# A mixture-of-experts stage on one core: rows for experts 4 to 31 fetched from DRAM through a slot table, in place of one-hot matmuls

## The chip, the cores and the metric

The kernel runs on one core of one Trainium2 chip. The metric is device time in microseconds (us) of one execution, lower is better; the time before is the median of three runs. A profile shows one further execution, with its own time.

## The reference, cut to what matters

Two blocks follow each other on 512 tokens of width 1024. The change touches only the end of the second block, the mixture of 32 experts. With `x` the residual stream and `h = rms_norm(x, norm_ffn)`:

```python
g_idx = argmax(softmax(h @ w_router_group))          # one of 4 groups
top_logit, top_idx = top_k(h @ w_router_expert[g_idx], 2)   # 2 of its 8 experts
gate = softmax(top_logit) * p_group[g_idx]
for each chosen expert e of a token:
    hid = silu(h @ w1[e]) * (h @ w3[e])              # 1024 -> 512
    y += gate * (hid @ w2[e])                        # 512 -> 1024
x = x + y
```

So 512 x 2 = 1024 token-expert pairs fall on 32 experts: 32 on average.

## The kernel before, in words

All matmuls run on float32 data that is split in two parts: a high part (`wh`, a cast on ACT, `piece_hi`) and a low part (`wl`, the difference, on DVE, `piece_lo`). An expert's weights come from DRAM as six 1 MB transfers, issued by SP, into a ring of buffers (`raw`, `pre`, `X`). Each transfer holds two *pieces*; an expert has 12 pieces (four each of w1, w3, w2), and the list `pieces` sets the order. For each piece the loop at the end of `build` runs PE's matmuls, with ACT and DVE splitting up to four pieces ahead; one w1 piece of each expert from expert 1 on is used unsplit (`whole`). Each expert has 64 slots (`CAP`) for its tokens. Its input `xg` holds 64 columns of high parts and 64 of low parts.

PE, DVE, ACT and POOL keep the order in which the code is written here (`manual_schedule`). Hooks (`after(i, d, f)`) put an expert's later steps behind a given piece: `s_copy1/3` and `s_add1/3` gather the two column halves, `s_hidden` makes the hidden layer, and `s_combine` (`combine`, L1509) multiplies by the gate into the tile `xs0`, of which there is one, and adds the 64 rows to the output by an indirect transfer on POOL's queue (L1517). Empty slots go to 64 spare rows behind the output.

**Gather.** For four experts at a time, `Gather` makes one-hot matrices on DVE (`start`, L1128), multiplies the token rows `hm` by them on PE (`sums`, `psc<-OH,X`), copies the result into `xg` on ACT and DVE (`step`, L1321 and L1323) and gets gates and row numbers by further small matmuls (`finish`). Group 0 is gathered in the router; the groups 1 to 7 while the last expert of the group ahead runs.

**Router.** For each of four token tiles m, between the matmuls of the last projection (`co`): `r_add`, `r_norm`, `r_rstd`, `r_scale`, `r_high`, `r_low` make the normalised rows and their two parts; `r_transpose`, `r_logits`, `r_choice` (some 12 small DVE operations), `r_place`, `r_place2` and `one_hot` find each token's experts and slots. POOL takes the low parts of the six first pieces and of two tiles.

```python
if e % NE == 3 and n != "w2" and e < 31:
    after(i, 0, lambda e=e: grp[e // NE + 1].step())
```

A loop at the end serves experts with more than 64 tokens; in the profiled execution PE has no instruction behind the last expert's.

## Time and profile before

| | |
|---|---|
| median of 3 runs | 1729.56 us (1728.92 to 1729.67) |
| the profiled execution's own time | 1727.33 us |
| its span, first to last instruction | 1725.4 us |
| PE, DVE, ACT, POOL busy | 95%, 75%, 51%, 10% of the span |
| mean granted TensorE clock | 0.987 |
| DRAM traffic | 336 MB, 308.69 MB of it on SP's queue |

Busy shares are means over stages. Up to about 1140 us the first block, attention and router run; from there to the end the experts do. A matmul's end is modelled and overlaps the next one's start. Times are us from the span's start unless marked ns.

### The profile page before, as it was taken

What the parts mean: (1) busy time and instruction counts of PE and PEld (TensorE: products, weight loads), DVE (VectorE), ACT (ScalarE), POOL (GpSimd) and SP (SyncE); (2) the same over time, 40 slices, a digit from 0 to 9 for tenths busy, and PEclk for the clock granted to TensorE, in tenths of its full rate; (3) what the DMA queues carried; (4) which work ended last, traced back from release to release, by engine and by line L of the source; (5) the groups of instructions that cost most, each with busy time, mean ns of one, the idle gap of its engine ahead of it and who ended that gap; (6) DMA issues with size and microseconds to landing.
All of it is one profiled execution on the core that took longest, in us unless ns stands there. A gap on an engine that the chain in (4) does not pass through costs nothing. (4 is left out here: it accounts for less than half of the span.)

```text
span 1725.4 us, 21422 instructions
## 1 busy us (share of the span) xinstructions
PE 1646.7 (95%) x8035; PEld 1325.1 (77%) x8035; DVE 1297.0 (75%) x1938; ACT 882.2 (51%) x1381; POOL 166.0 (10%) x146
## 2 busy tenths in 40 slices
PE   8999999999999999998999999889999999999995
PEld 6788888888888888887787877677676776777763
DVE  5969996489994465456656554579999999999995
ACT  6533232322223235343554432457878878778784
POOL 1100100000000000003101100320101101011011
PEclk9999999999999999998999999989999999999998
DMA  9932232223222362332212312429999999999994
GB/s 352 317 102 97 80 110 80 98 88 99 100 86 78 119 218 98 122 134 97 74 50 105 116 49 98 171 98 332 364 349 405 350 391 365 348 406 346 389 366 148
DMA packets 97801, 336.24 MB, mean 195 GB/s; under 512 B 6560, under 2 KB 24224, under 8 KB 73376
## 3 DMA queue, kind: packets, MB, share of 16 engines
q1 hardware_dynamic: 89952, 308.69, 47.2%
q0 software_dynamic: 6880, 23.96, 5.3%
q10 hardware_dynamic: 864, 2.21, 0.3%
q8 instruction: 64, 1.05, 0.2%
q14 instruction: 41, 0.34, 0.1%
HBM read 319.89 MB, written 14.94 MB: 194 GB/s over the span
## 5 line engine op out<-in xcount | busy, mean ns | idle before, releaser
L149 ACT CAST wh<-raw 128x1024 fp32r<-128x1024 f32 x174 | 182.0, 1051 | 386.0 <-PE ps L141 340.6
L150 DVE TENSOR_TENSOR wl<-raw,wh 128x1024 fp32r<-128x1024 f32 x174 | 212.4, 1224 | 170.0 <-ACT wh L149 169.1
L141 PE MATMUL pmm<-wh,X 128*128 128x512 f32 (+1 forms) x576 | 188.3, 398 | 2.3 <-ACT jk L784 1.8
L141 PE MATMUL ps<-hH,wl 128*128 128x512 f32 x448 | 175.2, 392 | 0.0
L141 PE MATMUL ps<-hL,wh 128*128 128x512 f32 x448 | 174.6, 390 | 0.5 <-DVE hL L150 0.5
L141 PE MATMUL ps<-hH,wh 128*128 128x512 f32 x448 | 174.5, 389 | 0.0
L487 DVE SCALAR_TENSOR_TENSOR cvo<-apad,cw,cvo 128x512 f32<-128x512 f32 x240 | 170.6, 757 | 0.9
L1257 DVE TENSOR_TENSOR wl<-raw,wh 128x1024 fp32r<-128x1024 f32 x137 | 163.4, 1222 | 3.0 <-ACT wh L1254 2.3
L141 PE MATMUL pmm<-wl,xr 128*128 128x512 f32 x322 | 138.4, 430 | 14.6 <-DVE wl L1257 14.6
L1254 ACT CAST wh<-raw 128x1024 fp32r<-128x1024 f32 x139 | 142.4, 1052 | 0.0
L1257 DVE TENSOR_TENSOR wl<-pre,wh 128x1024 fp32r<-128x1024 f32 x109 | 127.4, 1221 | 5.1 <-ACT wh L1254 5.1
L141 PE MATMUL pmm<-wh,xr 128*128 128x512 f32 x322 | 127.1, 395 | 0.0
L141 PEld LDWEIGHTS pmm<-wh,X 128*128 128x128 f32 x576 | 108.8, 195 | 22.6 <-ACT jk L784 2.0
L141 PE MATMUL ps<-wl,hH 128*128 128x512 f32 x320 | 124.5, 390 | 0.0
L141 PE MATMUL ps<-wh,hH 128*128 128x512 f32 x320 | 124.5, 389 | 0.0
L141 PE MATMUL ps<-wh,hL 128*128 128x512 f32 x320 | 124.5, 390 | 0.0
L141 PE MATMUL pmm<-wl,X 128*128 128x512 f32 (+1 forms) x288 | 114.3, 397 | 0.0
L1517 POOL DMA_INDIRECT out_dram<-xs,ii x31 | 64.2, 2070 | 505.7 <-DVE xs L1516 505.7
L1254 ACT CAST wh<-pre 128x1024 fp32r<-128x1024 f32 x113 | 112.0, 1055 | 0.0
L141 PEld LDWEIGHTS ps<-hL,wh 128*128 128x128 f32 x448 | 84.1, 188 | 18.4 <-DVE hL L150 0.9
L141 PEld LDWEIGHTS ps<-hH,wh 128*128 128x128 f32 x448 | 84.1, 188 | 17.5
L141 PEld LDWEIGHTS ps<-hH,wl 128*128 128x128 f32 x448 | 84.0, 188 | 17.5 <-issue 0.2
(426 smaller groups left out, 3431.2 us busy)
## 6 DMA issues: line engine op xcount, KB each, us to landing
raw<-in_w_dram SPq DMA_DIRECT2D x93, 1024.0 KB, 8.3
pre<-in_w_dram SPq DMA_DIRECT2D x62, 1024.0 KB, 7.7
raw<-in_w_in_dram SPq DMA_DIRECT2D x43, 1024.0 KB, 5.0
X<-in_w_dram SPq DMA_DIRECT2D x31, 1024.0 KB, 7.6
adar<-in_w_ada_dram SPq DMA_DIRECT2D x16, 512.0 KB, 8.5
raw<-in_w_in_dram SPq DMA_DIRECT2D x16, 512.0 KB, 4.5
raw<-in_w_ret_out_dram SPq DMA_DIRECT2D x8, 1024.0 KB, 4.9
raw<-in_w_out_dram SPq DMA_DIRECT2D x8, 1024.0 KB, 5.2
```

The lines of the kernel that those rows point to most:

```text
L141: PE.matmul(o, l, r, start=start, stop=stop)
L149: A.copy(hi, src)
L150: E.tensor_sub(lo, src, hi.bitcast(F32))
L487: V.scalar_tensor_tensor(st["o"], ap[:, j:j + T], cw[:, k, j:j + 1], st["o"], op0=OP.mult, op1=OP.add)
L1254: A.copy(split_of[i][0], raw_of[i])
L1257: E.tensor_sub(split_of[i][1], raw_of[i], split_of[i][0].bitcast(F32))
L1517: G.indirect_dma_start(out=out, out_offset=bass.IndirectOffsetOnAxis(ap=idx[:, :1], axis=0), in_=y[:64, :], in_offset=None, bounds_check=T ...
```

## The change

- The normalised rows (`r_scale` now on ACT with a strided read, `r_gain` on DVE) are also stored to DRAM (`xscr`); their order by feature is set once, so `r_high` and `r_low` read and write without strides.
- The router's lines stand in another order, and POOL no longer takes low parts: DVE does. Pieces 2 and 3 are used unsplit.
- `places` computes for each token and choice its slot, `table` writes row number and gate into the DRAM table `slots` by eight indirect transfers of 128 entries of 8 bytes, and reads the table back into `tb`.
- For experts 4 to 31, `fetch` gets the rows by an indirect transfer (POOL's queue, two experts ahead, two buffers), `turn` transposes them on PE, `parts` splits them on ACT and DVE. Groups 1 to 7 of the one-hot gather are gone.
- The scatters and fetches leave out slots that hold no token. Three buffers that held `hm` join the ring of weight buffers (nine in place of six).

Cut to what matters:

```diff
@@ -236,6 +238,8 @@
     sinT = hp.tile([128, T], F32, name="sinT")
     kscr = dp.tile([128, 2048], F32, name="kscr")
     vscr = dp.tile([128, 2048], F32, name="vscr")
+    xscr = dp.tile([T, D], F32, name="xscr")
+    slots = dp.tile([CAP * 32, 2], F32, name="slots")
...
@@ -1114,10 +1118,15 @@
-    g_ffn = gain(I["norm_ffn_2"].unsqueeze(0))
+    g_ffn = gain(I["gffn"])
     zero = alt("xs")
     V.memset(zero[:64], 0.0)
     G.dma_start(out[T:T + 64, :], zero[:64])
+
+    none = zero[:, 512:512 + CAP * 32 // 64].rearrange("p (s v) -> p s v", v=2)
+    V.memset(none, 0.0)
+    V.memset(none[:, :, 0].bitcast(I32), 1 << 20)
+    G.dma_start(slots.rearrange("(p s) v -> p s v", p=128), none)
     rt = [{} for m in range(NT)]
     rb = []
     NE = 4
@@ -1153,24 +1162,27 @@
         rt[m]["rs"] = sp.tile([128, 1], F32, name="rs1")
         rstd(rt[m]["rs"], rt[m]["ss"], D, 1e-6)
-    def r_scale(m, E=V):
-        rs = rt[m]["rs"]
-        E.scalar_tensor_tensor(rt[m]["xs"], xr[m], rs, g_ffn, op0=OP.mult, op1=OP.mult)
-
-
-    def natural(ap):
-        return ap.rearrange("t (c p k) -> t c p k", c=2, k=4)
     def by_feature(ap):
-        return ap.rearrange("t (c k p) -> t c p k", c=2, k=4)
+        return ap.rearrange("t (c p k) -> t c k p", c=2, k=4)
+
+    def tiles(ap):
+        return ap.rearrange("t (c k p) -> t c k p", c=2, k=4)
+
+    def r_scale(m):
+        A.activation(tiles(rt[m]["xs"]), by_feature(xr[m]), AF.Copy, scale=rt[m]["rs"])
+
+    def r_gain(m):
+        V.tensor_mul(rt[m]["xs"], rt[m]["xs"], g_ffn)
+        nc.scalar.dma_start(xscr[m * 128:m * 128 + 128, :], rt[m]["xs"])
     def r_high(m):
         h = xslot([128, 2, D])
-        A.copy(by_feature(h[:, 0]), natural(rt[m]["xs"]))
+        A.copy(h[:, 0], rt[m]["xs"])
         hm.append(h)
-    def r_low(m, E=V):
-        E.tensor_sub(by_feature(hm[m][:, 1]), natural(rt[m]["xs"]), by_feature(hm[m][:, 0].bitcast(F32)))
+    def r_low(m):
+        V.tensor_sub(hm[m][:, 1], rt[m]["xs"], hm[m][:, 0].bitcast(F32))
     def r_logits(m):
         b = rb[0][:, m * 40:m * 40 + 40]
@@ -1362,87 +1374,85 @@
     rb.append(ppv())
     cb = [pmm(), pmm(), pmm()]
+
+    for i in range(2):
+        piece_hi(i)
+        piece_lo(i, V)
     co(0, cb[0], 0)
     co(0, cb[0], 1)
     r_add(0, cb[0])
     r_norm(0)
     r_rstd(0)
-    piece_hi(0)
-    piece_lo(0, G)
+    co(1, cb[1], 0)
+    co(1, cb[1], 1)
     r_scale(0)
+    r_gain(0)
+    r_add(1, cb[1])
+    r_norm(1)
+    r_rstd(1)
+    r_transpose(0)
+    co(2, cb[2], 0)
     r_high(0)
     r_low(0)
-    co(1, cb[1], 0)
-    co(1, cb[1], 1)
-    r_add(1, cb[1])
-    r_transpose(0)
-    r_norm(1)
-    r_rstd(1)
+    r_logits(0)
     r_scale(1)
-    r_high(1)
-    piece_hi(1)
-    r_low(1)
-    piece_lo(1, G)
-    co(2, cb[2], 0)
+    r_choice(0)
...
+    r_gain(2)
+    r_rstd(3)
+    r_high(2)
+    r_scale(3)
+    g0 = group(0, OH0)
+    for n in ("pg", "pa"):
+        g0.begin(len(g0.begun), pget(n))
     r_choice(2)
-    r_scale(3)
-    piece_hi(4)
-    piece_lo(4, G)
-    r_high(3)
-    r_low(3, G)
-    piece_hi(5)
-    piece_lo(5, G)
     r_logits(3)
-    g0 = group(0, OH0)
-    g0.begin(0, pget("pg"))
+    for n in ("pg", "pa", "py", "py"):
+        g0.begin(len(g0.begun), pget(n))
     r_place(2)
     r_place2(2)
     one_hot(OH0, 2, pm1[:, 2, :NE])
-    for n in ("pg", "py", "py", "pa", "pa"):
-        g0.begin(len(g0.begun), pget(n))
+    r_low(2)
+    for k in range(6):
+        g0.more(g0.begun[k], k, 0, NT - 2)
     r_choice(3)
-    for k in range(2):
-        for l in range(2):
-            g0.more(g0.begun[k], k, l, NT - 2)
+    for k in range(6):
+        g0.more(g0.begun[k], k, 1, NT - 2)
+    r_gain(3)
+    r_high(3)
     r_place(3)
-    for k in range(2, 6):
-        for l in range(2):
-            g0.more(g0.begun[k], k, l, NT - 2)
     r_place2(3)
     one_hot(OH0, 3, pm1[:, 3, :NE])
+    r_low(3)
+    piece_hi(4)
+    piece_lo(4, V)
+    piece_hi(5)
+    piece_lo(5, V)
     p6.close()
     ex = mt_("ex", NT, 4)
     ge = mt_("ge", NT)
@@ -1461,10 +1471,39 @@
+    tb = mt_("tb", 32, 2)
+    dat = mt_("dat", NT, 2, 2)
+    pqv = mt_("pqv", NT, 2)
+    pen = mt_("pen", NT, 2)
+    pi = mt_("pi", NT, 2, dtype=I32)
+
+    def places():
+
+        w32 = late_[:, 384:].rearrange("p (m e) -> p m e", m=NT)
+        V.tensor_sub(el, Mb, o2)
+        for c, o in enumerate((el, o2)):
+            V.tensor_mul(w32, o, pm1)
+            V.tensor_reduce(pqv[:, :, c], w32, AX.X, OP.add)
+        V.tensor_scalar(pen, pqv, float(CAP), float(1 << 20), OP.is_gt, OP.mult)
+        V.tensor_scalar(pqv, pqv, 32.0, -32.0, OP.mult, OP.add)
+        V.tensor_add(pqv, pqv, gi[:, :, :2])
+        V.tensor_add(pqv, pqv, pen)
+        V.tensor_copy(pi, pqv)
+
+    def table():
+        for c, o in enumerate((gs, ge)):
+            V.tensor_copy(dat[:, :, c, 0].bitcast(I32), meta[:, :, 0])
+            V.tensor_copy(dat[:, :, c, 1], o)
+        for m in range(NT):
+            for c in range(2):
+                G.indirect_dma_start(out=slots, out_offset=bass.IndirectOffsetOnAxis(ap=pi[:, m, c:c + 1], axis=0),
+                                     in_=dat[:, m, c, :], in_offset=None, bounds_check=CAP * 32 - 1, oob_is_err=False)
+        for l in range(2):
+            G.dma_start(tb[l * 64:l * 64 + 64], slots.rearrange("(s e) v -> s e v", e=32))
     def up(b, x, k0, w):
@@ -1482,7 +1521,8 @@
     def whole(i):
-        return pieces[i][0] == "w1" and pieces[i][2] == 2 and pieces[i][1] > 0
+        n, e, c = pieces[i]
+        return n == "w1" and (c == 2 or e == 0 and c == 3)
     def down(yb, hd, f, w):
@@ -1515,7 +1555,7 @@
             A.activation(y[:64, c], yb[q][:64], AF.Copy, scale=gate[:64])
             V.scalar_tensor_tensor(y[:64, c], yb[q][64:], gate[64:], y[:64, c], op0=OP.mult, op1=OP.add)
         G.indirect_dma_start(out=out, out_offset=bass.IndirectOffsetOnAxis(ap=idx[:, :1], axis=0),
-                             in_=y[:64, :], in_offset=None, bounds_check=T + 63, oob_is_err=True,
+                             in_=y[:64, :], in_offset=None, bounds_check=T - 1, oob_is_err=False,
                              compute_op=OP.add)
     p6 = ExitStack()
@@ -1523,7 +1563,6 @@
     for n in ("q0", "q1"):
         raws.add((pre2, n, RAW, F32))
     raws.add((lp, "X0", RAW, F32))
-    grp = {0: g0}
     g0.step(4)
     st = [{} for e in range(32)]
     late = {}
@@ -1537,13 +1576,12 @@
             if raws.i == 10 and len(raws.slots) == 8:
                 p6.close()
                 raws.slots, raws.i = [raws.slots[j] for j in (2, 3, 4, 7, 0, 1)], 0
+                raws.slots = [((lp, f"X{j}", RAW, F32),) for j in (1, 2, 3)] + raws.slots
                 xp2 = p6.enter_context(pool("xg2", side="right"))
                 k = wsp.i % len(wsp.slots)
                 wsp.slots, wsp.i = wsp.slots[k:] + wsp.slots[:k], 0
                 wsp_add((xp2, "wh7"), (xp2, "wl7"))
                 wsp.slots = wsp.slots[-1:] + wsp.slots[:-1]
-                xgs.add((xp2, "xg4", [128, KT, 128], F32R))
-                xgs.i = 4
             piece_load(i)
         if not whole(i):
             piece_hi(i)
@@ -1567,9 +1605,38 @@
         st[e]["hd"] = hidden(st[e]["b"])
     def s_combine(e):
-        g = grp[e // NE]
         y = xgs.next().rearrange("p k t -> p (k t)").bitcast(F32) if e == 31 else None
-        combine(st[e]["y"], g.mg[:, e % NE:e % NE + 1], g.ii[:, e % NE:e % NE + 1], y)
+        if e < NE:
+            gate, ids = g0.mg[:, e:e + 1], g0.ii[:, e:e + 1]
+        else:
+            gate, ids = tb[:, e, 1:2], tb[:64, e, 0:1].bitcast(I32)
+        combine(st[e]["y"], gate, ids, y)
+
+    def fetch(o, ids):
+
+        G.indirect_dma_start(out=o, out_offset=None, in_=xscr, in_offset=bass.IndirectOffsetOnAxis(ap=ids, axis=0),
+                             bounds_check=T - 1, oob_is_err=False)
+
+    def turn(x):
+
+        b = pget("pg")
+        for k in range(KT):
+            transpose(b[:, k * 64:k * 64 + 64], x[:, k * 128:k * 128 + 128])
+        return b.rearrange("p (k s) -> p k s", k=KT)
+
+    def parts(b, xg):
+        A.copy(xg[:, :, :64], b)
+        V.tensor_sub(xg[:, :, 64:], b, xg[:, :, :64].bitcast(F32))
+
+    def s_fetch(e):
+        fetch(rows[:64, e % 2], tb[:64, e, 0:1].bitcast(I32))
+
+    def s_turn(e):
+        st[e]["xb"] = turn(rows[:64, e % 2])
+
+    def s_parts(e):
+        st[e]["xg"] = xgs.next()
+        parts(st[e]["xb"], st[e]["xg"])
@@ -1598,22 +1665,29 @@
         while done < len(pieces) and done < i + look:
             prepare(done)
             done += 1
-        g = grp[e // NE]
+        g = g0
         s_ = st[e]
+        if e < NE:
+            s_["xg"] = g.xg[e]
         if i in (1, 2):
             g.step(2)
         if i == 3:
+            places()
             gates()
+        if i == 4:
+            rows = lp.tile([128, 2, D], F32, name="X4")
+            G.memset(rows[:64], 0.0)
+            table()
         if i == 11:
             g.finish()
         if n != "w2":
             if c == 0:
                 s_[n] = pget("pa")
             if whole(i):
-                up_whole(s_[n], g.xg[e % NE], 2 * c, raw_of[i])
+                up_whole(s_[n], s_["xg"], 2 * c, raw_of[i])
             else:
-                up(s_[n], g.xg[e % NE], 2 * c, split_of.pop(i))
+                up(s_[n], s_["xg"], 2 * c, split_of.pop(i))
         else:
             if c == 0:
                 s_["y"] = [pget("pg" if e == 31 else "py") for _ in range(2)]
@@ -1634,13 +1708,12 @@
             after(i, 1, blocks)
             after(i, 5, blocks_before)
-        if e % NE == 2 and n == "w3" and c == 3 and e < 28:
-            grp[e // NE + 1] = group(e // NE + 1)
-            after(i, 1, grp[e // NE + 1].start)
-        if e % NE == 3 and n != "w2" and e < 31:
-            after(i, 0, lambda e=e: grp[e // NE + 1].step())
-            if n == "w3" and c == 3:
-                after(i, 1, grp[e // NE + 1].finish)
+        if n == "w1" and e < 32:
+            if c == 1 and NE <= e + 1 < 32:
+                after(i, 0, lambda e=e: s_turn(e + 1))
+                after(i, 1, lambda e=e: s_parts(e + 1))
+            if c == 3 and NE <= e + 2 < 32:
+                after(i, 0, lambda e=e: s_fetch(e + 2))
         for f in late.pop(i, ()):
             f()
     p8.close()
@@ -1679,8 +1752,9 @@
         ev = nc.sync.value_load(curi[0:1, 0:1], min_val=0, max_val=31)
         ga = Gather(pl, mt2, 2, 1, xgs.next)
         ga.start()
-        ga.step(8)
         ga.finish()
+        fetch(rows[:64, 0], ga.ii[:, 0:1])
+        parts(turn(rows[:64, 0]), ga.xg[0])
         w1, w3, w2 = (I[n][bass.ds(ev, 1)].rearrange("o k n -> (o k) n") for n in ("w1_2", "w3_2", "w2_2"))
         aS = lp.tile([128, 2, 512], F32, name="gain0")
         b = pget("ph")
```

Three places of the order that the code sets.

DVE, at the step from one expert to the next, in the last expert of a group, before (`xs` is the combined output, `xr` the next group's input, the others weight parts):

```order
L1503 TENSOR_TENSOR hs<-hs,ppv 128x256
L150 TENSOR_TENSOR hd<-hs,hd 128x4x64
L1516 SCALAR_TENSOR_TENSOR xs_9740<-ptr,mg,xs_9740 64x512 x2
L1321 CAST xr_9699<-psc 128x128
L1321 CAST xr_9700<-psc 128x128
L1257 TENSOR_TENSOR gain_9764<-raw_9761,xs_9763 128x1024
L1321 CAST xr_9699<-psc 128x128
L1321 CAST xr_9700<-psc 128x128
```

and the same place now, in any expert (`L1629` is `parts`):

```order
L1543 TENSOR_TENSOR hs<-hs,ppv 128x256
L152 TENSOR_TENSOR hd<-hs,hd 128x4x64
L1556 SCALAR_TENSOR_TENSOR xs_9261<-ptr,mg,xs_9261 64x512 x2
L1269 TENSOR_TENSOR wl_9272<-raw_9269,wh_9271 128x1024
L1269 TENSOR_TENSOR wl_9289<-raw_9269,wh_9288 128x1024
L1629 TENSOR_TENSOR xr_9294<-psc,xr_9294 128x8x64
```

One 512-column subtraction in every expert stands in place of sixteen 128-column casts and four one-hot operations in every fourth.

POOL, in the router, before (`wl` are the first pieces' low parts, `X` the tiles' low parts, `rs` the small power for the norm):

```order
L1257 TENSOR_TENSOR wl_8315<-pre_8213,wh_8314 128x1024
L225 TENSOR_TENSOR rs_8381<-rs_8381,mhalf 128x1
L1173 TENSOR_TENSOR X_8385<-xs_8378,X_8385 128x2x128x4
L1257 TENSOR_TENSOR wl_8435<-pre_8215,wh_8434 128x1024
L225 TENSOR_TENSOR rs_8460<-rs_8460,mhalf 128x1
L1257 TENSOR_TENSOR wl_8439<-pre_8215,wh_8438 128x1024
```

POOL has only the `rs` rows there now. Behind them, from piece 4 on, stands the table, with the semaphores that each waits for (DMASW are those of POOL's transfers, each number used in turn):

```order
L1680 MEMSET X_8726 64x2048 [waits DVE_49,PE_49]
L1503 DMA slots<-dat,pi 2048x2 [waits DMASW5_49,DVE_49]
L1503 DMA slots<-dat,pi 2048x2 [waits DMASW6_49,DVE_49]
L1503 DMA slots<-dat,pi 2048x2 [waits DMASW7_49]
L1503 DMA slots<-dat,pi 2048x2 [waits DMASW1_49,DMASW0_49]
...
L1503 DMA slots<-dat,pi 2048x2 [waits DMASW4_49]
L1506 DMA tb<-slots 64x64 [waits DMAHW5_49,DMASW5_49]
L1506 DMA tb<-slots 64x64
L1557 DMA out_dram<-xs_8975,ii 576x1024 [waits DMAHW4_49,DMAHW7_49,DMAHW2_49,DVE_49]
L1617 DMA X_8726<-xscr,tb 64x1024 [waits DMAHW4_49,DMAHW3_49,DMAHW5_49,DMASW6_49,Pool_49]
```

Each write to `slots` waits for the one before it to land, the reading back for the last of them; expert 0's scatter and expert 4's fetch come behind on the same queue.

## Rows read from the trace of the kernel before

**Rows 1.** Windows, the router's end: busy us by engine, clock, DMA share, GB/s.

```profile
core 0: us, PE busy (x) PEld busy (x) DVE busy (x) ACT busy (x) POOL busy (x), PEclk, DMA share, GB/s
1100.00:1150.00 50.00, 36.67 (x203) 33.22 (x203) 36.51 (x92) 21.12 (x36) 19.50 (x9) 0.80 0.37 147
```

**Rows 2.** Windows: four experts (10 to 13) singly, then experts 2 to 30.

```profile
1359.00:1374.70 15.70, 15.45 (x69) 11.07 (x67) 14.98 (x16) 13.36 (x18) 2.26 (x1) 1.00 0.95 354
...
1374.70:1390.30 15.60, 14.52 (x65) 10.60 (x64) 14.89 (x15) 13.26 (x18) 2.26 (x1) 1.00 1.02 396
...
1390.30:1407.30 17.00, 15.95 (x78) 11.84 (x76) 16.28 (x19) 13.32 (x19) 2.25 (x1) 1.00 1.01 410
...
1407.30:1429.80 22.50, 22.15 (x146) 18.67 (x146) 19.66 (x38) 16.63 (x33) 1.40 (x1) 1.00 0.90 337
...
1217.68:1706.62 488.94, 466.43 (x2368) 354.60 (x2366) 454.68 (x577) 392.33 (x572) 58.10 (x29) 1.00 0.95 366
```

**Rows 3.** Waits, 1288 to 1712 us, SP's queue: total us, times, longest.

```profile
SPq L1248 <- DVE wl L1257: 157.9, 72, 4.3
```

**Rows 4.** Timeline of DVE, 1363 to 1374 us: start, us, what, idle before.

```profile
1363.53 4.62 DVE L1257 TENSOR_TENSOR wl<-pre,wh 128x1024 fp32r<-128x1024 f32 x4
...
1368.07 1.22 DVE L1257 TENSOR_TENSOR wl<-raw,wh 128x1024 fp32r<-128x1024 f32 x1
...
1373.07 1.54 DVE L1516 SCALAR_TENSOR_TENSOR xs<-ptr,mg,xs 64x512 f32<-64x512 f32 x2 [0.16 <-ACT xs L1515]
```

**Rows 5.** Groups by form, 1288 to 1712 us, five gathers: busy, mean ns.

```profile
L141 PE MATMUL psc<-OH,X 128*128 128x256 f32 x320 | 47.5, 287 | 1.8 <-ACT xr L1323 1.4 <-ACT xg L1323 0.3
...
L1321 DVE CAST xr<-psc 128x128 fp32r<-128x128 f32 x64 | 16.2, 285 | 2.7 <-ACT xr L1323 1.9 <-ACT xg L1323 0.6
...
L1128 DVE TENSOR_TENSOR OH<-cst,pm 128x256 fp32r<-128x256 f32 x20 | 7.1, 424 | 0.0
```

**Rows 6.** Groups by form, DVE, then ACT, 1040 to 1150 us.

```profile
L1083 DVE TENSOR_TENSOR X<-ppv,X 128x512 fp32r<-128x512 f32 x3 | 2.1, 688 | 2.7 <-ACT X L1082 2.7
...
L1169 ACT CAST X<-xs 128x1024 fp32r<-128x1024 f32 x4 | 8.1, 2013 | 12.7 <-DVE xs L1158 12.7
...
L1082 ACT CAST X<-ppv 128x512 fp32r<-128x512 f32 x3 | 1.8, 587 | 6.8 <-PE ppv L141 6.8
```

**Rows 7.** DMA view, 1390.3 to 1407.3 us: packets, MB, share of 16 engines.

```profile
q1 hardware_dynamic: 924, 6.71, 93.7%
q0 software_dynamic: 80, 0.26, 7.7%
```

**Rows 8.** Timelines of the router: DVE, POOL and PE.

```profile
1108.26 0.24 DVE L1195 TENSOR_SCALAR o<-cst,gi 128x32 f32<-128x32 f32 x1
...
1113.11 2.84 DVE L1195 TENSOR_SCALAR o<-cst,gi 128x32 f32<-128x32 f32 x1
...
1149.88 0.17 DVE L1453 TENSOR_TENSOR ex<-lg,v 128x16 f32<-128x16 f32 x1
...
1113.06 2.85 POOL L1173 TENSOR_TENSOR X<-xs,X 128x1024 fp32r<-128x1024 f32 x1 [3.37 <-ACT X L1169]
...
1119.31 3.61 PE L141 MATMUL ppv<-gain,OH 128*128 128x40 f32 x16 [7.90 <-DVE pm L1211]
...
1142.48 0.63 PE L141 MATMUL pmm<-wl,xr 128*128 128x512 f32 x1
```

**Rows 9.** Timeline of POOL: the scatters of experts 1 and 2.

```profile
1195.27 1.42 POOL L1517 DMA_INDIRECT out_dram<-xs,ii  x1 [14.92 <-DVE xs L1516]
1217.68 2.26 POOL L1517 DMA_INDIRECT out_dram<-xs,ii  x1 [20.99 <-DVE xs L1516]
```

**Rows 10.** DMA issues on POOL's queue, whole run: KB, us to landing.

```profile
ascr<-cvo POOLq DMA_DIRECT2D x8, 256.0 KB, 2.6
...
out_dram<-xs,ii POOLq DMA_INDIRECT x31, 8.6
...
out_dram<-xr,ii POOLq DMA_INDIRECT x1, 4.8
```

More of the change, by code (lines that the diff above doesn't have):

```diff
@@ L86, in layouts @@
     d["rows"] = np.concatenate([np.asarray(inp[n]).reshape(-1) for n in R_SPEC])[None]
+    d["gffn"] = np.ascontiguousarray(
+        np.asarray(inp["norm_ffn_2"]).reshape(2, 128, 4).transpose(0, 2, 1).reshape(1, D))
     d["onorm"] = np.concatenate([np.asarray(inp["out_norm_attn_2"]), np.asarray(inp["out_norm_sgu_2"])])[None]
@@ L1369, in build @@
     r_rstd(0)
-    piece_hi(0)
-    piece_lo(0, G)
+    co(1, cb[1], 0)
+    co(1, cb[1], 1)
     r_scale(0)
+    r_gain(0)
[4 more added lines that the diff above has]
+    co(2, cb[2], 0)
     r_high(0)
     r_low(0)
-    co(1, cb[1], 0)
-    co(1, cb[1], 1)
-    r_add(1, cb[1])
-    r_transpose(0)
-    r_norm(1)
-    r_rstd(1)
-    r_scale(1)
-    r_high(1)
-    piece_hi(1)
-    r_low(1)
-    piece_lo(1, G)
-    co(2, cb[2], 0)
+    r_logits(0)
+    r_scale(1)
+    r_choice(0)
     co(2, cb[2], 1)
-    r_logits(0)
+    r_gain(1)
     r_add(2, cb[2])
     r_transpose(1)
-    r_choice(0)
     r_norm(2)
     r_rstd(2)
-    r_scale(2)
-    r_high(2)
-    r_low(2, G)
     b = pmm()
     co(3, b, 0)
+    r_high(1)
+    r_low(1)
     r_transpose(2)
     r_logits(1)
+    r_scale(2)
     r_choice(1)
-    piece_hi(2)
-    piece_lo(2, G)
-    piece_hi(3)
     co(3, b, 1)
+    r_place(0)
+    r_place(1)
     r_add(3, b)
-    r_place(0)
-    r_place2(0)
     r_norm(3)
-    r_rstd(3)
     r_logits(2)
     r_transpose(3)
-    piece_lo(3, G)
     OH0 = mp.tile([128, NT + 1, NE, 64], F32R, name="OH", bufs=2)
     V.memset(OH0[:, NT].bitcast(F32), 0.0)
-    r_place(1)
-    r_place2(1)
     for m in range(2):
+        r_place2(m)
         one_hot(OH0, m, pm1[:, m, :NE])
-    r_choice(2)
-    r_scale(3)
-    piece_hi(4)
-    piece_lo(4, G)
-    r_high(3)
-    r_low(3, G)
-    piece_hi(5)
-    piece_lo(5, G)
+    r_gain(2)
[5 more added lines that the diff above has]
+        g0.begin(len(g0.begun), pget(n))
+    r_choice(2)
     r_logits(3)
-    g0 = group(0, OH0)
-    g0.begin(0, pget("pg"))
+    for n in ("pg", "pa", "py", "py"):
+        g0.begin(len(g0.begun), pget(n))
     r_place(2)
@@ L1463, in gates @@
         V.memset(meta[:, :, 1:2], 1.0)
-        V.tensor_sub(el, Mb, o2)
         V.tensor_mul(el, el, bc(gs, 32))
@@ L1707 @@
 _INS = ["x", "positions", "w_ada", "w_in", "w_ret_out", "w_conv_out", "w_out", "mem_2", "norm_mix_2", "w_in_2",
-        "w_out_2", "norm_cross_2", "w_cq_2", "w_ck_2", "w_cv_2", "w_co_2", "norm_ffn_2", "w1_2", "w3_2", "w2_2"]
+        "w_out_2", "norm_cross_2", "w_cq_2", "w_ck_2", "w_cv_2", "w_co_2", "w1_2", "w3_2", "w2_2"]
 def kernel(**inputs):
```

## The prediction

> **What bounds the kernel now.** I read the busy table and the slices of the page first: PE is busy 95% of the span, but a matmul's modelled end overlaps the next, so that share says little. The windows say more. The whole stretch from expert 2's scatter to expert 30's is 488.94 us for 28 experts, 17.46 us each, with 366 GB/s from DRAM [rows 2]. It repeats in groups of four: 15.7, 15.6, 17.0 and 22.5 us. In the first three DVE is busy 14.98 of 15.70, 14.89 of 15.60 and 16.28 of 17.00 us, PE waits for it now and then, and SP's queue, which refills the weight buffers, waits for DVE's reads of them (158 us, 72 times) [rows 2, 3]. In the fourth, which gathers the next group, PE is busy 22.15 of 22.50 us, DVE 19.66: there PE ends last [rows 2].
>
> DVE's fast period can be counted. Four splits of 1024 columns start at 1363.53 and the next at 1368.07: 1.135 us apart [rows 4]. Eleven of them are 12.5 us. The hidden layer, the combine (1.54 us [rows 4]) and their short waits fill the other 3.15 us of 15.65. The third expert's extra 1.4 us is the one-hot work, four operations of 424 ns, partly overlapped [rows 5].
>
> Ahead of the experts lies the router's end, where the granted clock is 0.80 on average, so part of the time at the lower of its two levels (1.2 and 2.4 GHz), and PE is busy 36.67 of 50 us [rows 1]. PE stood idle 7.90 us before the logits at 1119.31 [rows 8].
>
> **The change, term by term** (negative is time saved).
>
> *Gathers 1 to 7 go.* PE loses 64 matmuls of 256 columns and their like per group, DVE sixteen casts of 285 ns and the one-hots [rows 5]. Each expert gains one `parts`: a 512-column subtraction from PSUM on DVE. The nearest row is 688 ns busy [rows 6]; back to back such rows lose 0.08 us to overlap, as the splits do (1.22 busy, 1.135 apart [rows 4]), so I take 0.61. The cast on ACT, 587 ns [rows 6], lies beside it: ACT is busy 13.3 of 15.6 us [rows 2]. PE's eight small transposes are not in the trace; between nothing and the 287 ns of a 256-column matmul [rows 5] they are 0 to 2.3 us, and PE, which then needs some 14.5 us (second line of [rows 2]), still stays under DVE even at the upper end, if barely. DVE's period becomes 15.65 + 0.61 = 16.26 us; I take 16.35 for small waits. 28 experts: 457.8 against 488.94, **-31.1**. From expert 1's scatter to expert 2's the same step was 1217.68 - 1195.27 = 22.4 us with a gather [rows 9]: **-6.1**. The one-hots in front of expert 1's combine: **-1.4**.
>
> *Is DRAM fast enough?* In the third window 6.71 MB of weights took 93.7% of 17.0 us and the 64-row scatter (0.26 MB) 7.7%, 1.31 us [rows 7]. An expert's 6.29 MB of weights are then 14.9 us. A scatter holds 1024/32 = 32 rows on average once empty slots go: 0.65 us. The fetch of 32 rows is between its bytes at the weights' rate, 0.3 us, and the scatter's price, 0.65. The sum is 15.9 to 16.2 us, just below DVE's 16.26; that is why I add only 0.1. These are 6.55 MB per expert, 403 GB/s, and 410 GB/s stands in the third window [rows 2]. The Trainium skill, DMA: Bandwidth & Descriptors, section Specifications, gives a limit of about 358 GB/s from HBM per core. By it an expert would need 18.3 us, an estimate, and the stretch would get longer; this trace's 410 GB/s over 17 us speaks against it.
>
> *The fetch's own wait.* It is issued ten pieces, about 13.6 us, before `turn` needs it. The scatter, with twice the rows, lands in 8.6 us [rows 10], so the fetch is hidden with 5 us to spare. It stands on POOL behind a scatter that is issued three pieces earlier; POOL is busy some 2.3 us for one [rows 2].
>
> *Router.* POOL's low parts go: while one ran at 1113.06 for 2.85 us, a DVE operation that takes 0.24 us took 2.84 [rows 8]. POOL is busy 19.5 of these 50 us [rows 1]; I put 11 of them on the chain. DVE gets in return two contiguous low parts and two pieces, some 4 us at 1.135 each. ACT's strided pass over a tile, 2.01 us before [rows 6], only moves from `r_high` to `r_scale`. Following the new order by hand from the last `co` (PE free at 1111), with these durations, the first expert matmul, now at 1142.48 [rows 8], starts near 1135.5: **-7**, with -2 to -12 as its bounds, since order by hand misses waits.
>
> *Places and table on DVE*: fourteen small operations of some 0.2 us, as the 0.17 and 0.24 us rows [rows 8], **+2.8**, on a DVE that is the bound. Pieces 2 and 3 unsplit cost PE about 0.4 us each beside that, nothing on DVE.
>
> *The table on POOL's queue.* This is the change's new wait. The gates stand at 1149.88 now [rows 8]; with -7, `places` and one split more, the eight writes start near 1150. Each waits for the one before to land. Behind the last come the reading back, then expert 0's scatter, then expert 4's fetch. `combine` has one tile `xs0`, so ACT cannot write expert 1's combine until expert 0's scatter has read it; casts and, soon, DVE stand behind ACT. Expert 1's combine is due at 1195.3 - 7 + 2.8 - 1.4 = 1189.7. With s for one write, the tile is free at 1150 + 8s + 9 (about 2 us to issue, 7 to land with half the rows), so the stall is 8s - 30.7. The trace has no indirect write of 8 bytes. Below, a plain 256 KB store on POOL's queue lands in 2.6 us; above, the scatter under load takes 8.6 [rows 10]. The nearest is the last scatter, indirect and without load, 4.8 us [rows 10]; these writes carry 1 KB but run beside weights, so I take s = 5.6: **+14**, with 0 and +38 as ends. A delayed fetch for expert 4 lands about as the stall ends and adds nothing of size.
>
> The rest is unchanged or hidden: initialising `slots` and storing `xscr` lie in a stretch with DMA share 0.37 [rows 1]; POOL's `memset` of the rows ends before the table starts; the tail behind expert 30 has the same steps.
>
> Sum: -31.1 - 6.1 - 1.4 - 7 + 2.8 + 14 = **-28.8 us** against the profiled execution's own 1727.33, that is 1698.5. That execution is 2.2 us below the median of the runs, so for the runs I forecast 1729.56 - 28.8 = 1701.
>
> **Rivals.**
>
> *Short chain (22%).* If a small write lands in under 3.8 us, the stall is nil. For it speaks the 2.6 us store, against it that this store has no load beside it. Time: 1701 - 14 = 1687. The Trainium skill, DMA: Bandwidth & Descriptors, section Anatomy of one DMA — SWDGE (gpsimd) path, fits 2.0 us plus bytes at 436 GB/s for a transfer from GpSimd's queue: by that rule the eight take 16 us, an estimate, and this rival holds. For the last scatter's 256 KB the same rule gives 2.6 us, and the trace shows 4.8.
>
> *Long chain (13%).* Each write takes the loaded scatter's 8.6 us: stall 38, time 1725. The table's stretch is loaded, but the writes are small.
>
> *Transfers become the bound (8%), on the other side.* DVE no longer pauses for a gather every fourth expert, and with nine buffers SP always has a free one. If DRAM gives only the stretch's mean of 366 GB/s [rows 2], an expert takes 6.55 MB / 366 = 17.9 us, 28 take 501, +43 on the forecast: 1744, slower than before. It decides above 17.4 us per expert, below 377 GB/s. For it: DMA share 1.01 in the second and third windows, so no time was left there. Against it: 396 and 410 GB/s in the same windows, with scatters of twice the rows.
>
> *The rows do not come in time (3%).* Then the change does not do what it says: PE waits at each `turn`. It decides beyond 13.6 us from issue to landing; at 15 us, +1.4 us on each of 28: 1740. The scatter's 8.6 us speaks against it.
>
> **How the numbers follow.** The forecast, a chain of 4.5 to 7 us a write and DVE's period, has 52%; the cases above 22, 13, 8 and 3; 2% is left for what I don't see. About 0.2%, 3.5 us, is what a measurement of this kernel can tell from no change. The forecast, the short chain and most of the long one are faster: 88%. Within 0.2% I put the long chain's far end and a weak form of slow transfers: 5%. Slower: 7%. The range runs from the short chain with a router 5 us better, 1682, to the long chain, 1725. The single number is that of the likeliest case.
>
> **What would show it.** Right: combines 16.2 to 16.5 us apart from expert 4 on, DVE busy over 90% and no wait of ACT for weights; eight `slots` transfers of 5 to 6 us each, one behind the other; one wait of ACT of some 14 us before expert 1's combine; no DVE operation of the router stretched, first expert matmul near 1136. Wrong: ACT's casts wait for weight transfers (DRAM is the bound), PE waits at `turn` in every expert, or the gap before expert 1's combine is nil or over 35 us.

## The result and the profile after

The changed kernel takes 1709.78 us, median of four runs (1706.31 to 1712.25), beside 1729.62 for the kernel before on the same chip: ratio 0.9885, 95% interval 0.9873 to 0.9897. 1701 was forecast, faster with a chance of 0.88, between 1682 and 1725. The profiled execution took 1708.95 us, 18.4 less than that of before; the sum had said 28.8.

The windows of the kernel after. In a row: window and its length, busy time of PE, PEld, DVE, ACT and POOL, granted clock, DMA share, GB/s.

```profile
1100.00:1150.00 50.00, 42.09 (x240) 34.61 (x241) 37.41 (x127) 27.54 (x46) 5.27 (x5) 0.93 0.55 203
1150.00:1200.00 50.00, 34.52 (x179) 26.45 (x177) 32.72 (x48) 27.62 (x35) 19.24 (x12) 0.87 0.70 256
1300.00:1400.00 100.00, 98.43 (x447) 66.79 (x445) 95.03 (x99) 85.30 (x113) 19.53 (x12) 1.00 1.02 399
1500.00:1600.00 100.00, 93.87 (x426) 63.97 (x425) 91.13 (x95) 80.72 (x105) 17.47 (x12) 1.00 1.02 392
```

The first row answers to [rows 1]: POOL is busy 5.27 us where it was 19.50, PE 42.09 where it was 36.67, and the clock is 0.93 where it was 0.80. In the second PE is idle a third of the time. In the third DVE is busy 95%, in the fourth only 91% while the DMA share stays at 1.02: something other than DVE holds the loop there.

The timeline of POOL of the kernel after, at the table and the first scatters (start, duration, what was issued, idle time before it and what ended it):

```profile
1147.95 3.21 POOL L1503 DMA_INDIRECT slots<-dat,pi  x1 [7.11 <-DVE dat L1500]
1157.06 1.01 POOL L1503 DMA_INDIRECT slots<-dat,pi  x1 [5.90 <-DVE ix L1352]
1159.54 6.76 POOL L1503 DMA_INDIRECT slots<-dat,pi  x1 [1.47 <-DMA slots<-dat,pi]
1171.16 0.97 POOL L1503 DMA_INDIRECT slots<-dat,pi  x1 [4.86 <-DMA slots<-dat,pi]
1177.17 1.74 POOL L1503 DMA_INDIRECT slots<-dat,pi  x1 [5.05 <-DMA slots<-dat,pi]
...
1193.63 0.97 POOL L1503 DMA_INDIRECT slots<-dat,pi  x1 [1.41 <-DMA slots<-dat,pi]
1196.06 1.16 POOL L1506 DMA_DIRECT2D tb<-slots  x2 [1.46 <-DMA slots<-dat,pi]
1197.74 1.52 POOL L1557 DMA_INDIRECT out_dram<-xs,ii  x1 [0.52 <-DMA tb<-slots]
...
1203.93 2.29 POOL L1557 DMA_INDIRECT out_dram<-xs,ii  x1 [3.34 <-DVE xs L1556]
```

From the first write to the table's load 48.1 us pass, 6.0 per write on average; the single gaps are 2.4 to 11.6 us. The profile puts the second write's wait down to a DVE operation (`ix`) whose result it doesn't use; in e6's trace the same wait is put down to the first write's landing. Expert 0's scatter (L1557, with the row numbers `ii`) stands behind the load. The waits of ACT and of PE between 1140 and 1210 (us in total, times, longest):

```profile
ACT xs L1555 <- DMA out_dram<-xs,ii: 15.7, 1, 15.7
PE psc L230 <- DMA X<-xscr,tb: 16.5, 1, 16.5
```

Two waits, then, at the same time: ACT's combine of expert 1 waits for `xs0`, and PE's turn of expert 4 waits for its fetch.

From expert 4 on the scatters, on POOL's timeline, follow each other every 16.26 us; expert 3's is at 1237.75, and those of experts 19 to 22 are:

```profile
1497.96 2.28 POOL L1557 DMA_INDIRECT out_dram<-xs,tb  x1 [12.70 <-DVE xs L1556]
...
1514.35 2.28 POOL L1557 DMA_INDIRECT out_dram<-xs,tb  x1 [12.82 <-DVE xs L1556]
...
1531.64 2.28 POOL L1557 DMA_INDIRECT out_dram<-xs,tb  x1 [13.73 <-DVE xs L1556]
...
1549.13 2.28 POOL L1557 DMA_INDIRECT out_dram<-xs,tb  x1 [13.94 <-DVE xs L1556]
```

Sixteen steps from 1237.75 are 16.26 us on average; from expert 20 they are 17.3, 17.5, 17.7. Over expert 19 to 30 the steps are 10.1 us longer than as many of 16.26. About 1 us of that is expert 30's own step, 17.3 to 17.5 us in every run, the kernel before included. What is late there, by the waits of ACT from 1250 to 1690 (none of these before 1500):

```profile
ACT wh L1266 <- DMA X<-in_w_dram: 7.0, 7, 1.7
ACT wh L1266 <- DMA raw<-in_w_dram: 6.2, 5, 2.0
...
ACT wh L1266 <- DMA pre<-in_w_dram: 2.7, 2, 1.6
```

The casts wait for weights. The DMA queues in two stretches, from expert 4's scatter to expert 20's (260.33 us) and from there to expert 27's (121.72 us); q1 is SP's queue, q0 POOL's:

```profile
DMA packets 16189, 103.40 MB, mean 397 GB/s; under 512 B 3080, under 2 KB 3080, under 8 KB 4075
q1 hardware_dynamic: 13612, 99.10, 94.7%
q0 software_dynamic: 2560, 4.08, 6.7%
...
DMA packets 7339, 47.58 MB, mean 391 GB/s; under 512 B 1261, under 2 KB 1261, under 8 KB 1809
q1 hardware_dynamic: 6211, 45.24, 92.8%
q0 software_dynamic: 1120, 2.25, 8.5%
```

In the first, 99.10 / 16 = 6.19 MB of weights arrive per step where an expert uses 6.29; POOL's queue carries 0.255 MB per step. In the second it carries 0.32: the later experts hold more rows.

### The profile page after: what moved, and what is told of

Read it like the earlier page. It is cut to its first block, busy times and chain, and to the rows that moved or that the text cites. A ratio compares the mean times of both kernels' runs of the same rounds, so it can differ in the third digit from the quotient of the medians.

```text
span 1707.2 us, 20336 instructions
## 1 busy us (share of the span) xinstructions
PE 1618.5 (95%) x7587; PEld 1264.1 (74%) x7587; DVE 1267.9 (74%) x1805; ACT 877.2 (51%) x1299; POOL 199.1 (12%) x178
## 4 chain that ended last, share of the span: by engine, by line
issue 21%; PE 18%; DMA 15%; DVE 4%; POOL 2%; ACT 1%; POOLq 0%; ACTq 0%; DVEq 0%
DMA out_dram<-xs,tb 13%; PE pmm L143 9%; PE ps L143 4%; PE ppv L143 2%; DMA out_dram<-xs,ii 2%; PE psc L143 2%; PE ptr L230 1%; POOL rs L227 1%; POOL slots L1503 1%; DVE wl L152 0%; POOL sgw L831 0%; DMA adg<-in_w_ada_dram 0%; DVE xs L765 0%; ACT wh L1266 0%; DVE xr L796 0%
## 5 line engine op out<-in xcount | busy, mean ns | idle before, releaser
L151 ACT CAST wh<-raw 128x1024 fp32r<-128x1024 f32 x174 | 182.1, 1051 | 386.1 <-PE ps L143 341.7
L152 DVE TENSOR_TENSOR wl<-raw,wh 128x1024 fp32r<-128x1024 f32 x174 | 211.9, 1221 | 171.3 <-ACT wh L151 170.4
L143 PE MATMUL pmm<-wl,xr 128*128 128x512 f32 x388 | 175.3, 452 | 11.3 <-DVE wl L1269 9.7
L1269 DVE TENSOR_TENSOR wl<-X,wh 128x1024 fp32r<-128x1024 f32 x132 | 155.5, 1218 | 5.7 <-ACT wh L1266 5.4
L143 PE MATMUL pmm<-wh,xr 128*128 128x512 f32 x388 | 153.9, 397 | 0.0
L1266 ACT CAST wh<-X 128x1024 fp32r<-128x1024 f32 x132 | 133.2, 1053 | 7.1 <-DMA X<-in_w_dram 7.0
L1269 DVE TENSOR_TENSOR wl<-raw,wh 128x1024 fp32r<-128x1024 f32 x104 | 121.7, 1220 | 3.8 <-ACT wh L1266 3.5
L143 PEld LDWEIGHTS pmm<-wl,xr 128*128 128x128 f32 x388 | 73.4, 189 | 59.5 <-DVE wl L1269 39.8
L1266 ACT CAST wh<-raw 128x1024 fp32r<-128x1024 f32 x104 | 104.4, 1053 | 6.3 <-DMA raw<-in_w_dram 6.2
L1557 POOL DMA_INDIRECT out_dram<-xs,tb x27 | 61.6, 2281 | 355.6 <-DVE xs L1556 355.6
L143 PEld LDWEIGHTS ps<-hH,wh 128*128 128x128 f32 x448 | 84.3, 188 | 17.6
```

The costliest lines, as they stand in the source:

```text
L143: PE.matmul(o, l, r, start=start, stop=stop)
L151: A.copy(hi, src)
L152: E.tensor_sub(lo, src, hi.bitcast(F32))
L1266: A.copy(split_of[i][0], raw_of[i])
L1269: E.tensor_sub(split_of[i][1], raw_of[i], split_of[i][0].bitcast(F32))
L1557: G.indirect_dma_start(out=out, out_offset=bass.IndirectOffsetOnAxis(ap=idx[:, :1], axis=0), in_=y[:64, :], in_offset=None, bounds_check=T ...
```

## The experiments

Two questions: what bounds the loop, and what the table costs. Each run was timed against the kernel before on its own chip; ratios are to that.

| run | median us | ratio, 95% interval |
|---|---|---|
| changed kernel | 1709.78 | 0.9885 (0.9873 to 0.9897) |
| e1 no fetch from expert 6 | 1696.03 | 0.9814 (0.9802 to 0.9827) |
| e2 scatter all slots | 1716.30 | 0.9929 (0.9917 to 0.9941) |
| e3 second `xs0` | 1709.11 | 0.9884 (0.9870 to 0.9899) |
| e4 four tables | 1700.93 | 0.9838 (0.9824 to 0.9851) |
| e5 six buffers | 1715.41 | 0.9925 (0.9911 to 0.9939) |
| e6 ten buffers | 1705.10 | 0.9866 (0.9851 to 0.9881) |
| e7 four tables, ten buffers | 1697.90 | 0.9819 (0.9806 to 0.9833) |
| e8 two pieces unsplit | 1705.98 | 0.9868 (0.9853 to 0.9884) |
| e9 before, new router alone | 1717.60 | 0.9940 (0.9927 to 0.9954) |
| e10 before, empty slots left out | 1727.34 | 0.9992 (0.9983 to 1.0001) |
| e11 no fetch, experts 6 to 17 | 1700.36 | 0.9835 (0.9822 to 0.9849) |
| e12 e7 with a later merge | 1690.88 | 0.9781 (0.9767 to 0.9794) |

### What bounds the loop

**e1.**

```diff
-            if c == 3 and NE <= e + 2 < 32:
+            if c == 3 and NE <= e + 2 < NE + 2:
```

> The changed kernel without the fetches for experts 6 to 31 (that part of the computation is left out: these experts work on stale rows; everything else stays, the turn, the parts and the scatter). It moves 32 rows of 4 KB, 0.13 MB, less per expert. Theory A (from expert 20 on DRAM is the bound: 17.2 us between scatters in place of DVE's 16.26, and the 11 steps from expert 20 to 30 cost 10 us together): 6.42 MB in 16.26 us are 395 GB/s, what DRAM gave there, so the late steps go back to 16.26 and the time falls by 7 to 10 us, to 1700 to 1703. Rival B (the late steps are long for a reason other than bytes, on DVE, ACT or POOL): unchanged within 2 us, 1708 to 1712.

Ratio 0.9814, about 12 us less than the changed kernel. Expert 21's scatter and the next two, POOL's timeline of e1:

```profile
1528.40 2.26 POOL L1557 DMA_INDIRECT out_dram<-xs,tb  x1 [13.99 <-DVE xs L1556]
1544.67 2.27 POOL L1557 DMA_INDIRECT out_dram<-xs,tb  x1 [14.00 <-DVE xs L1556]
1560.92 2.26 POOL L1557 DMA_INDIRECT out_dram<-xs,tb  x1 [13.99 <-DVE xs L1556]
```

16.26 us up to expert 29, so 9.1 us of the long steps are gone (expert 2 to 30: 456.3 us, 465.4 in the changed kernel). The DMA queues of e1 over sixteen steps from expert 4's scatter on:

```profile
DMA packets 15123, 102.77 MB, mean 395 GB/s; under 512 B 2361, under 2 KB 2361, under 8 KB 2816
...
q1 hardware_dynamic: 13826, 100.69, 94.8%
```

100.69 / 16 = 6.29 MB per step, just what an expert uses. The loop is DVE's while the weights keep up, and DRAM's when they don't. The rest lies, in the traces, ahead of expert 2 (2.0 us) and behind expert 30 (2.2 us); it wasn't expected. The first part is no more than executions of the same code differ by: with nothing changed ahead of it, expert 0's scatter stands at 1195.71 us here, at 1197.74 in the changed kernel and at 1199.98 in e11.

**e2.** The scatters of 64 slots again:

```diff
-                             in_=y[:64, :], in_offset=None, bounds_check=T - 1, oob_is_err=False,
+                             in_=y[:64, :], in_offset=None, bounds_check=T + 63, oob_is_err=False,
...
+            V.tensor_scalar(to, tb[:64, :, 0].bitcast(I32), cst[:64, C_PIX + 1:C_PIX + 2], None, OP.min)
```

> The changed kernel with the scatters of all 64 slots again (empty slots to the 64 spare rows, as before the change; one small DVE operation makes the row numbers). The fetch still leaves empty slots out. Twice the rows per scatter: 0.13 MB more, 0.65 us of all transfer engines by the price in the trace of before. Theory A (DRAM has hardly anything left beside DVE's 16.26 us): the reserve of nine buffers is used up much earlier and most of 28 experts grow by 0.4 to 0.65 us: plus 6 to 16 us, 1716 to 1726. Rival B (DVE bounds the loop, transfers lie beside it): plus 0 to 2 us, 1710 to 1712.

7 us more, at the lower end. The long steps begin behind expert 11 in place of 19:

```profile
1352.78 2.28 POOL L1557 DMA_INDIRECT out_dram<-xs,jk  x1 [12.71 <-DVE xs L1556]
...
1369.04 2.28 POOL L1557 DMA_INDIRECT out_dram<-xs,jk  x1 [12.70 <-DVE xs L1556]
...
1385.67 2.28 POOL L1557 DMA_INDIRECT out_dram<-xs,jk  x1 [13.08 <-DVE xs L1556]
```

**e10.** The same edit on the kernel before (the first line of e2's diff, the other way round).

> The kernel before with nothing but the empty slots left out of the scatters (a bound of T - 1 on the row number, no error beyond it). 0.13 MB less per expert on a kernel whose expert loop takes 17.46 us each at 366 GB/s. Theory A (DRAM is no bound there on the mean): within 1.5 us of the kernel before, 1727 to 1730. Rival: the scatters' half of 1.31 us counts in the three fast steps of each group, where the transfer engines' share was 1.01: minus 5 to 13 us, 1716 to 1724.

0.9 us, not to be told from nothing. So one edit is worth 7 us in the new loop and nothing in the old, which takes 17.46 us an expert and lets the transfers catch up in its fourth step (337 GB/s there, [rows 2]).

**e5 and e6.** Without the line that adds X1 to X3 to the ring, and with one buffer more:

```diff
-                raws.slots = [((lp, f"X{j}", RAW, F32),) for j in (1, 2, 3)] + raws.slots
+                raws.slots = [((lp, f"X{j}", RAW, F32),) for j in (1, 2, 3)] + [((xp2, "X5", RAW, F32),)] + raws.slots
```

> The changed kernel with the ring of six weight buffers, as before the change (the three buffers that held hm stay unused). Theory A: from 1254 to 1514 us the weights arrived at 6.19 MB per expert where 6.29 are used, so a reserve of some 1.6 MB is used up over 16 experts and DRAM is the bound only then; with three buffers (3.1 MB) less there is no reserve and the steps are 16.6 to 17.3 us from expert 4 on: plus 5 to 14 us, 1715 to 1724. Rival B (the buffers are not what decides, as DVE's period hides the loads): plus 0 to 2 us, 1709 to 1712.

> The changed kernel with a tenth weight buffer of 1 MB. Theory A: it is filled in the stretch ahead of 1200 us, where the transfer engines are busy only 0.7 of the time, and the deficit of 0.1 MB per expert then lasts for some ten experts more, so the steps stay 16.26 us to the end or nearly: minus 6 to 10 us, 1700 to 1704. Rival B: one buffer more changes nothing (the late steps are DRAM's rate alone, whatever was loaded ahead): 1708 to 1711.

Six: some 6 us more, the first long step behind expert 8 (16.95 us). Ten: 3 to 5 less, half of what was expected, and in the traces only 2.3 us of it lie between expert 2 and 30 (463.2 against 465.4). In the 88 us up to expert 2's scatter SP's queue moved 24.02 MB, 1.2 more than with nine buffers (22.80), but the long steps began only one expert later. A reserve matters; its size in MB doesn't give the size of the gain.

**e11.**

```diff
-            if c == 3 and NE <= e + 2 < 32:
+            if c == 3 and NE <= e + 2 < 32 and not NE + 2 <= e + 2 < 18:
```

> The changed kernel without the fetches for experts 6 to 17 (left out: these experts work on stale rows); experts 4, 5 and 18 to 31 fetch theirs. The steps up to expert 19 were DVE's 16.26 us in any case. Theory R (a reserve of weights in the buffers is used up over all experts): about 1.4 MB more stand in the buffers at expert 18, so the long steps behind expert 20 come later or go: 4 to 8 us less, 1702 to 1706. Rival L (the long steps come from the experts 18 to 27 themselves, whose fetches and scatters carry more rows, 0.30 to 0.40 MB per step where experts 2 to 15 carry 0.15 to 0.30): the long steps stay as they are, 1708 to 1711.

Ratio 0.9835, some 9 us less: theory R, and more than it said; between expert 2 and 30 the trace is 6.8 us shorter (458.6 against 465.4). Experts 20 to 24, which fetch their rows, now step at 16.27 us. The DMA queues from expert 19's scatter to expert 20's show what the rows of these experts still cost:

```profile
q1 hardware_dynamic: 805, 5.84, 91.5%
q0 software_dynamic: 160, 0.40, 9.8%
```

5.84 MB of weights arrive where 6.29 are used; the rest comes from what was loaded ahead. So both hold: the later experts draw the reserve down faster, and whether that is felt depends on what the earlier ones left.

**e8.**

```diff
-        return n == "w1" and (c == 2 or e == 0 and c == 3)
+        return n == "w1" and (c in (1, 2) if e else c > 1)
```

> The changed kernel with two pieces of w1 unsplit per expert in place of one: DVE has one split of 1.135 us less per expert, ACT one cast less, PE some 0.4 us more. Theory A: DRAM gives 397 GB/s and an expert's 6.4 to 6.55 MB take 16.2 to 16.5 us, so a DVE period of 15.1 only empties the reserve sooner: minus 3 to plus 3 us, 1707 to 1713. Rival B (DVE alone sets the loop): 18 to 28 steps of 15.1 us, minus 18 to 30 us, 1680 to 1692.

3 to 4 us less: 1 us beyond theory A, and far from rival B. The windows of e8, early and late in the loop:

```profile
1250.00:1300.00 50.00, 50.00 (x233) 36.66 (x231) 46.85 (x50) 42.32 (x56) 12.13 (x8) 1.00 1.02 402
1500.00:1600.00 100.00, 96.06 (x411) 62.01 (x411) 82.32 (x87) 73.83 (x98) 18.90 (x12) 1.00 1.02 389
```

Early, PE is busy all the time and the step is 15.53 us: with one split less PE sets it, so what set 16.26 was DVE, although PE is busy 98% there. From expert 10 on the steps grow, to 17 us and more, with DVE at 82%. Expert 2 to 30 takes 464.8 us, as with more work on DVE (465.4). In this loop a faster DVE buys next to nothing. The 3 to 4 us lie ahead of expert 0's scatter, at 1194.55 us; whether the edit or the spread told at e1 puts it there isn't shown.

### What the table costs

**e3.**

```diff
-        y = xgs.next().rearrange("p k t -> p (k t)").bitcast(F32) if e == 31 else None
+        y = rows[64:, e // 2 % 2] if e < 31 and e % 2 else xgs.next().rearrange("p k t -> p (k t)").bitcast(F32) if e == 31 else None
```

> The changed kernel with a second tile for combined rows: odd experts use the idle half (partitions 64 to 127) of the tile that the fetches write. Expert 1's combine no longer waits for expert 0's scatter to read xs0. Theory: the wait of 15.7 us before expert 1's combine is only one of two waits that end together, since expert 4's turn on PE waits for its fetch behind the same queue until 1202.65 us; the gap moves to the turn and the time stays within 3 us, 1707 to 1713. Rival: the single xs0 is what the table's chain costs: minus 10 to 15 us, 1695 to 1700.

Nothing, 0.9884. ACT's wait for `xs0` is gone; PE's is where it was:

```profile
PE psc L230 <- DMA X<-xscr,tb: 16.3, 1, 16.3
```

Of two waits that end together, taking one away brings nothing. (From expert 4 on every second step of e3 is 16.44 us, 2.2 us over the loop, so a gain of that size could hide behind it; the rival's 10 to 15 could not.)

**e4 and e7.** Four tables, and e7 with the tenth buffer:

```diff
-    slots = dp.tile([CAP * 32, 2], F32, name="slots")
+    slots = [dp.tile([CAP * 32, 2], F32, name=f"slots{j}") for j in range(4)]
...
+        for c in range(2):
+            for m in range(NT):
+                G.indirect_dma_start(out=slots[m], ...
...
+        for j in range(4):
+            G.dma_start(tq[:, j], slots[j].rearrange("(s e) v -> s e v", e=32))
+    def merge():
...
+        V.tensor_reduce(ti, q[:, :, :, 0], AX.X, OP.min)
+        for l in range(2):
+            V.tensor_reduce(tg[l * 64:l * 64 + 64], q[:, :, :, 1], AX.X, OP.add)
```

> The changed kernel with four tables in place of one, one per token tile: the eight small indirect writes no longer wait for each other, except the second choice for the first in the same table; four loads bring the tables back, and DVE merges them (minimum of the row numbers, sum of the gates, three small operations). Theory: the chain of 48 us from the first write to the table's load is 8 landings one behind the other; with two landings in a row it is 15 to 28 us, the load is done before expert 0's scatter, the stall of some 15 us goes and the scatters of experts 0 and 1 come 15 us earlier; then 1694 to 1698, or, since DRAM is idle in the stall and must give the same bytes later, up to 5 us of it given back, 1699 to 1702. Rival: the writes take 6 us each because POOL or the queue works them off one by one whatever their table is: the chain stays over 40 us and the time at 1706 to 1713.

> Four tables and ten buffers together. Theory: the two gains lie in different stretches (the step from expert 0 to 2, and the steps behind expert 20), so they add: 1700.9 for four tables alone, less 6 to 10, 1691 to 1695. Rival: without the pause the reserve isn't filled, and what the tenth buffer brings is lost again: 1698 to 1702.

8 us less than the changed kernel, and with ten buffers 11. e4 lies in its theory's second case (1699 to 1702), but not for that case's reason, as the rows below show; e7 gains less than its theory and stands at the edge of its rival. POOL's timeline of e4, and a wait of DVE:

```profile
1145.60 3.20 POOL L1505 DMA_INDIRECT slots<-dat,pi  x1 [7.10 <-DVE dat L1502]
1149.10 1.38 POOL L1505 DMA_INDIRECT slots<-dat,pi  x1 [0.30 <-issue]
1150.79 0.97 POOL L1505 DMA_INDIRECT slots<-dat,pi  x1 [0.30 <-issue]
...
1171.68 1.03 POOL L1508 DMA_DIRECT2D jk<-slots  x2 [2.56 <-DMA slots<-dat,pi]
1179.44 2.36 POOL L1565 DMA_INDIRECT out_dram<-xs,ii  x1 [6.74 <-DVE xs L1564]
```

```profile
DVE ti L1512 <- DMA jk<-slots: 8.4, 1, 8.4
```

The writes no longer wait for each other, and the last load is issued 26 us after the first write. What was not gained went into a new wait: DVE reached the merge before the tables did. It isn't lost to DRAM: in e4 the steps of experts 20 to 30 take 171.8 us, in the changed kernel 172.5.

**e12.** e7 with the merge and expert 4's fetch later:

```diff
-        if i == 20:
+        if i == 26:
             merge()
...
-                after(i, 0, lambda e=e: s_fetch(e + 2))
+                after(i, 3 if e == 2 else 0, lambda e=e: s_fetch(e + 2))
```

> Four tables and ten buffers, with the merge of the tables and expert 4's fetch six and three pieces later. With four tables DVE sat 8.4 us before the merge, as the tables landed only at 1175 us; PE then waited 11.3 us for a split. Theory: with the merge behind six more pieces that wait goes and the scatters of experts 0 to 20 come 8 us earlier; the DRAM side gives part of it back since it must bring the same bytes: 1690 to 1694. Rival: all of it is given back in the late steps: 1697 to 1699.

1690.88 us, ratio 0.9781: faster than both kernels. Against e6, with the same buffers but one table, that is 1705.1 - 1690.9 = 14.2 us: the price of the chain. The window from 1150 to 1200 of e12:

```profile
1150.00:1200.00 50.00, 46.75 (x234) 33.43 (x233) 44.97 (x61) 40.38 (x52) 24.35 (x16) 1.00 0.94 338
```

PE is busy 46.75 us where it was 34.52 in the changed kernel, the clock is 1.00 where it was 0.87, and the transfers, too, use time that they had let pass (0.94 against 0.70).

**e9.** The router's lines alone, in the kernel before.

```diff
-    piece_hi(0)
-    piece_lo(0, G)
+    co(1, cb[1], 0)
+    co(1, cb[1], 1)
     r_scale(0)
+    r_gain(0)
...
```

> The kernel before with the router's new order alone (row scaling on ACT, low parts on DVE, pieces 2 and 3 of expert 0 unsplit); the one-hot gather of all groups, the scatters of 64 slots, six buffers, no table. Theory: the first expert matmul comes 9.0 us earlier in the changed kernel's trace, and nothing behind it needs that time: minus 7 to 10 us, 1719 to 1722. Rival: the experts' first stretch waits for weight transfers, so an earlier start is lost there: minus 0 to 3 us, 1726 to 1729.

Ratio 0.9940, 10.7 us less, just beyond the 7 to 10 expected. The scatters of experts 1 and 2, POOL's timeline of e9:

```profile
1185.61 1.43 POOL L1520 DMA_INDIRECT out_dram<-xs,ii  x1 [14.91 <-DVE xs L1519]
1208.02 2.26 POOL L1520 DMA_INDIRECT out_dram<-xs,ii  x1 [20.99 <-DVE xs L1519]
```

Both stand 9.7 us ahead of [rows 9]; nothing behind takes it back. Which part of the router's edit brings it (the order, POOL's low parts, the strides or the unsplit pieces) no run separates.

## Why the prediction was right, and where its sizes were off

Its direction held, and its mechanisms up to expert 20; behind that its own rival, the transfers, bounds the loop. The profiled executions split as follows (negative is saved):

| stretch | forecast | measured |
|---|---|---|
| to the first expert matmul | -7 | -9.0 (1142.48 to 1133.51) |
| from there to expert 1's scatter | +15.4 | +17.6 (52.79 to 70.42) |
| expert 1's scatter to 2's | -6.1 | -4.9 (22.41 to 17.56) |
| expert 2's to 30's | -31.1 | -23.5 (488.94 to 465.40) |
| behind expert 30's | 0 | +1.5 |

*DVE's period* was right: 15.65 + 0.61 = 16.26 was worked out (the sum took 16.35), and 16.26 is what sixteen steps of the kernel and nearly every step of e1 show. `parts` takes 692 ns beside the 688 of [rows 6]. PE's transposes take 0.7 us per expert (11.3 us for 128 of them in the sixteen steps). That PE stays under DVE even at their upper end of 2.3 us was a slip: 14.5 + 2.3 = 16.8 is above 16.26.

*"Is DRAM fast enough?"* is the step that failed. The loop took 7.6 us more than forecast: 9.1 of waits for weights, which e1 takes away, and 1.0 that e1 keeps (expert 30's step), less the 2.5 by which 28 steps of 16.26 undercut 16.35. It set 15.9 to 16.2 us of transfers against 16.26 of DVE and added 0.1. Two inputs were off. It leaned on 410 GB/s, which stood in one window of 17 us [rows 2], with 396 in its neighbour; sixteen steps of the new loop got 397. And it took 32 rows for every expert, where POOL's queue carries 0.15 to 0.30 MB per step up to expert 15 and up to 0.40 from there on. The rival "transfers become the bound" came true in a weak form, in the last third of the loop: its signs are there (ACT's casts wait for weights, which the prediction names as a sign of being wrong, and the DMA share is 1.02), at 17.4 us a step (121.72 / 7), where it put the point of no gain, but for some eight steps only. The Trainium skill, DMA: Bandwidth & Descriptors, section Specifications, states about 358 GB/s from HBM per core, as half of what a stack gives to two cores. For this kernel, on one core, that is no limit: it got 392 to 402 GB/s from 1250 to 1600 us.

*The table's chain* was the right new wait with nearly the right price: 5.6 us a write assumed, 6.0 measured; 14 us of stall forecast, 15.7 waited, 14.2 gained when e12 removes it beside e6. That the price came so near is partly luck: 6.0 is the mean of gaps of 2.4 to 11.6 us, not "5 to 6 us each". Expert 4's fetch landed as the stall ended, as forecast; so there were two waits of one length, and the single `xs0` was not by itself the price (e3). The short chain did not come: 48 us. The Trainium skill, DMA: Bandwidth & Descriptors, section Anatomy of one DMA — SWDGE (gpsimd) path, gives 2.0 us plus bytes for one transfer, by estimate 16 us for the eight. Only the three writes beside idle transfer engines, 2.4 to 2.5 us each, come near that.

*Places and table* took DVE 2.6 + 0.4 us by its timeline; +2.8 was said. *The router* gave 9 to 11 us, within its bounds of 2 to 12: the granted clock rose from 0.80 to 0.93 in its window, and the small operations on DVE take their 0.2 us. *The fetch* lands in about 8 us and PE waited for it once only, at expert 4; that rival stays out. *The tail* was to stay as it was, and the stretch behind the very last scatter grew from 12.5 to 15.0 us. The rows show no instruction that explains it. It is shorter with fewer fetches: with 28 of them 15.0 us, with 16 (e11) 14.0, with 2 (e1) 12.8, with none and no table (e10) 12.0. That it grows with the number of transfers on POOL's queue is a guess from these four; no run was made for it.
